# A gated linear-attention block: the second head's scores-times-values moved to the other two quarters of TensorE's array

## The chip, the cores and the metric

The kernel runs on one core of a Trainium2 chip. The metric is the device time of one execution in microseconds (us), as the median of several runs. The names of the engines in profiles are PE (TensorE's matmuls), PEld (TensorE's weight loads), DVE (VectorE), ACT (ScalarE), POOL (GpSimd) and SP (SyncE, which issues the DMAs).

## The reference, cut to what matters

One encoder block over 16 meta tokens and 1024 tokens with 1024 channels: a norm, a wide input projection, a pooling mixer, a gated linear attention, gates that merge the two, an output projection, and a squared-ReLU MLP. The change touches the attention. It has four heads with 64 key channels and 128 value channels, and goes in chunks of 64 tokens:

```python
def gla_chunk_step(S, inp):
    qc, kc, vc, ac = inp
    b = jnp.cumsum(ac, axis=2)
    decay = jnp.exp(-jnp.abs(b[:, :, :, None, :] - b[:, :, None, :, :]))
    scores = jnp.einsum('bhtk,bhsk,bhtsk->bhts', qc, kc, decay)
    o = jnp.einsum('bhts,bhsv->bhtv', scores, vc) + jnp.einsum('bhtk,bhkv->bhtv', qc * jnp.exp(b), S)
    b_end = b[:, :, -1:, :]
    S_new = jnp.exp(b_end[:, :, 0, :])[..., None] * S + jnp.einsum('bhsk,bhsv->bhkv', kc * jnp.exp(b_end - b), vc)
    return S_new, o
...
    o = rmsnorm(o, gla_norm.reshape(GLA_HEADS, GLA_DV)) * jax.nn.silu(r).reshape(B, L, GLA_HEADS, GLA_DV)
```

So the output o of a chunk is the masked and decayed scores times the values of the same chunk, plus the decayed queries times the state from the chunks before. It is normed over the 128 value channels of each head and multiplied by a gate made from r.

## The kernel before, in words

**Stages.** The program goes through the input projections for gates and queries (to about 208 us), the pooling mixer, then the attention (about 310 to 490 us), the merge with the output projection (to about 615 us) and the two MLP products (to the end). Most products of float32 operands are made as three matmuls of split operands (lines 255 to 257, the helper mm3); the attention's own are plain float32 matmuls, each of which the trace holds as two records of PE.

**The attention.** The heads go in pairs p (two heads e = 0, 1) and the tokens in halves of 512, so there are four units, in the order (0,0), (1,0), (0,1), (1,1) for (p, half). A unit has four token tiles j of 128, and each token tile has two chunks u of 64. A unit passes through `inside` (line 1210), which makes the masked scores `scc` level by level (score matmuls of line 1207 into the buffer b_sc, masked copies of line 1270), and then through `across` (line 1277). The `across` of one unit runs beside the `inside` of the next.

**The steps of `across`.** Line 1287 turns the decayed keys. Line 1296 multiplies keys by values into the two-bank buffer m2 (b_m in the trace), and line 1302 carries the states through the eight chunks on VectorE, reading that buffer. Line 1309 multiplies the scores by the values into the next b_m; since there is one such buffer, it waits for the last line 1302. Line 1314 (`seen`) reads one column of the result, so that the accumulation of line 1319 (queries times states, into the same places) comes after line 1309. Then come the squares (1328), their sums (1331), the norm's root (218 to 228), the multiply by it (1333), eight transposes to channels on partitions (1337), the multiply by the gate r in `sr` (1338, one instruction over 1024 columns), and the split of the product into two float32r parts for the merge (1340 on ScalarE, 1341 on VectorE).

**The quarters of the array.** All these matmuls have 64 rows of contraction and 64 columns of output. `tile_position=(row, column)` puts such a matmul on one 64 by 64 quarter of the array: the row says which partitions the operands come from, the column to which half of the partitions the result goes. In line 1309 the scores and values of chunk u lie on partition half u, and the result of token half u goes to partition half u, for both heads: positions (0, 0) and (64, 64). Lines 1207, 1296 and 1319 use all four positions in turn.

**The order of the work.** PE's order is written out in the program: `gla` (line 1344) steps through the generators, and each `yield us` pours as many microseconds of filler matmuls (key, value and gate projections, then the merge's products of `yb_block`, line 1088) before the next step. The other engines' orders are not written by hand at first, and are from `early_gates` (line 1073) on, which comes ahead of the last unit's `across`: from there ScalarE's and VectorE's instructions run in the order of the program. In that last stretch (the tail) the merge's products (lines 1115 and 1116, the rounding of line 1119, the remainder of lines 1121 and 1123 on VectorE or GpSimd) stand between the steps of the last unit, and the output weights (lines 1414, 1422, 1423) and the merge's weights (lines 83 and 87) are loaded and split.

Of the kernel before, what the change touches and what calls it, by code (L numbers as in the profile page):

```python
# [12 lines left out]
ALU = mybir.AluOpType  # L13
# [7 lines left out]
HALF = 512  # L21
CH = 64
# [92 lines left out]
def kernel(  # L115
# [10 lines left out]
    act, dve, pool, pe = nc.scalar, nc.vector, nc.gpsimd, nc.tensor  # L126
# [20 lines left out]
    def bank(tag):  # L147
        if tag in rota:
            turn_of[tag] = turn_of.get(tag, -1) + 1
            tag = rota[tag][turn_of[tag] % len(rota[tag])]  # L150
        return psp[tag].tile([P, 512], F32, name=f"b_{tag}", tag=tag)

    def two(tag):

        if tag == "sc":
            if "sc" not in wide:
                wide["sc"] = psp["sc"].tile([P, 2, 512], F32, name="b_sc", tag="sc")
            return wide["sc"]
        return psp[tag].tile([P, 2, 512], F32, name=f"b_{tag}", tag=tag)
# [40 lines left out]
    def f32(ap):  # L200
        return ap.bitcast(F32)
# [11 lines left out]
    def inv_sqrt(ss, n, inv, bias=None):  # L213

        rows, cols = ss.shape[0], n
        k = inv_sqrt.k = (inv_sqrt.k + 1) % 2
        v, y = stat[2 * k][:rows, 0:cols], stat[2 * k + 1][:rows, 0:cols]
        t = stat[2 * k][:rows, 8 : 8 + cols]
        act.activation(y, ss, ACT.Ln, scale=inv, bias=eps_t[:rows] if bias is None else bias)
        dve.tensor_scalar(v, ss, inv, EPS if bias is None else bias, ALU.mult, ALU.add)  # L220
        act.activation(y, y, ACT.Exp, scale=-0.5)
        if cols == 1:
            dve.scalar_tensor_tensor(t, v, y, y, ALU.mult, ALU.mult)
        else:
            dve.tensor_tensor(t, v, y, ALU.mult)
            dve.tensor_tensor(t, t, y, ALU.mult)
        dve.tensor_scalar(t, t, -0.5, 1.5, ALU.mult, ALU.add)
        dve.tensor_tensor(ss, y, t, ALU.mult)
        return ss
# [29 lines left out]
    def quad(a):  # L259
        return a.rearrange("p (k c) -> p k c", k=4)  # L260
# [934 lines left out]
    def part(i):  # L1195
        return slice(i * CH, (i + 1) * CH)
# [80 lines left out]
    def across(p, half):  # L1277


        v = S["v"][p][:, 4 * half : 4 * half + 4].rearrange("p j (e c) -> p j e c", e=2)  # L1280
        qe, kt, kl, W = (S[n] for n in ("qe", "kt", "kl", "W"))
        scc = S["scc"][:, p]
        dec = S["ends"][:, HALF - 2 * NC : HALF - NC]
        first = S["S"][:, half, p]
        yield 1.5
        b = quad(bank("ms"))
        for j in range(4):
            pe.transpose(b[:, j], kl[:, j * P : (j + 1) * P], ident)
        act.activation(kt, b, ACT.Copy)
        yield 1.6  # L1290
        while p and "v" not in done:
            yield 1.0
        kv = two("m2").rearrange("p u (j c) -> p u j c", j=4)
        for j in range(4):
            for u, e in ((0, 0), (1, 1), (1, 0), (0, 1)):
                pe.matmul(
                    kv[part(e), u, j], kt[part(u), j, part(e)], v[part(u), j, e], start=True, stop=True,
                    tile_position=(u * CH, e * CH),
                )
        states = [first] + [W[:, c] for c in range(NC - 1)] + ([S["S"][:, 1, p]] if half == 0 else [])  # L1300
        for c, dst in enumerate(states[1:]):
            dve.scalar_tensor_tensor(dst, states[c], dec[:, c : c + 1], kv[:, c % 2, c // 2], ALU.mult, ALU.add)
        yield 4.4

        o = two("m2").rearrange("p e (j c) -> p e j c", j=4)
        for j in range(4):
            for e in range(2):
                for u in range(2):
                    pe.matmul(  # L1309
                        o[part(u), e, j], scc[part(u), e, j], v[part(u), j, e], start=j == 0, stop=False,  # L1310
                        tile_position=(u * CH, u * CH), skip_group_check=True,
                    )

        dve.tensor_copy(seen, o[:, :, 3, P - 1])
        yield 0.8
        for j in (3, 0, 1, 2):
            for e, u in ((0, 0), (1, 1), (1, 0), (0, 1)):
                c = 2 * j + u
                pe.matmul(
                    o[part(u), e, j], qe[part(e), part(c)], states[c][part(e)], start=False, stop=True,  # L1320
                    tile_position=(e * CH, u * CH), skip_group_check=True,
                )
        while "v" not in done:
            yield 1.0
        sr = S["sr"].rearrange("p e t -> p (e t)")
        nc.sync.dma_start(sr.rearrange("p (e t) -> p e t", e=2), r_dram[2 * p : 2 * p + 2, half].rearrange("h p t -> p h t"))
        on, o = S["on"], o.rearrange("p e j c -> p (e j) c")
        act.activation(on, o, ACT.Square)
        ss = rms[rms_n[0] % 2]
        rms_n[0] += 1  # L1330
        dve.tensor_reduce(ss, on, AX.X, ALU.add)
        rs = inv_sqrt(ss, 8, 1.0 / P)
        dve.tensor_tensor(on, o, rs[:, :, None].broadcast_to([P, 8, P]), ALU.mult)
        yield 6.0
        b = two("m2").rearrange("p e (j c) -> p (e j) c", j=4)
        for j in range(8):
            pe.transpose(b[:, j], on[:, j], ident)
        dve.tensor_tensor(sr, b.rearrange("p a c -> p (a c)"), sr, ALU.mult)
        yh, yl = (S["yg"][half][:, n, 2 * p : 2 * p + 2].rearrange("p e t -> p (e t)") for n in range(2))
        act.activation(yh, sr, ACT.Copy)  # L1340
        dve.tensor_tensor(yl, sr, f32(yh), ALU.subtract)
        done.add((p, half))

    def gla():
# [16 lines left out]
        for n, u in enumerate(units + [None]):  # L1361
            if u is None:
                early_gates()
            live = side + old + ([inside(*u, units[n - 1] if n else None)] if u else [])
            while live:
                waits = [(g, next(g, None)) for g in live]
                live = [g for g, w in waits if w is not None]
                pour(max([w for _, w in waits if w is not None], default=0) * PACE)
                if not live:
                    break  # L1370
            if n == 2:
                done.add(("o", 0))
            if n == 0:
                while ("k", 1) not in done:
                    next(filler)
            old = [across(*u)] if u else []
            side = [meta_state(1)] if n == 0 else []
# [403 lines left out]
```

## Time and profile before

| | us |
|---|---|
| median of 3 runs | 1224.9 (1224.36 to 1225.51) |
| the profiled execution, its whole time | 1225.56 |
| its span | 1222.7 |
| PE busy | 1202.0 |
| VectorE busy | 853.9 |
| ScalarE busy | 618.9 |
| busy time of line 1309's matmuls, all four units | 7.86 |
| busy time of line 1319's matmuls, all four units | 4.42 |
| busy time of line 1338 on VectorE, all four units | 4.9 |

The profiled execution's time is its span and what lies around it. All times inside the program are counted from the span's start. Busy times of PE are modelled at their ends, since matmuls are pipelined. A row of the timeline reads: start, length, engine, line, operation, output <- inputs, shapes, count, and in brackets the idle time of the engine just before with what ended it. A row of a line's view reads: shortest, median and longest length in ns, then the first and last start.

### The profile page before, as it was taken

What the parts mean: (1) busy time and instruction counts of PE and PEld (TensorE: products, weight loads), DVE (VectorE), ACT (ScalarE), POOL (GpSimd) and SP (SyncE); (2) the same over time, 40 slices, a digit from 0 to 9 for tenths busy, and PEclk for the clock granted to TensorE, in tenths of its full rate; (3) what the DMA queues carried; (4) which work ended last, traced back from release to release, by engine and by line L of the source; (5) the groups of instructions that cost most, each with busy time, mean ns of one, the idle gap of its engine ahead of it and who ended that gap; (6) DMA issues with size and microseconds to landing.
All of it is one profiled execution on the core that took longest, in us unless ns stands there. A gap on an engine that the chain in (4) does not pass through costs nothing.

```text
span 1222.7 us, 18359 instructions
## 1 busy us (share of the span) xinstructions
PE 1202.0 (98%) x6818; PEld 1000.4 (82%) x6818; DVE 853.9 (70%) x1399; ACT 618.9 (51%) x1099; POOL 62.7 (5%) x100
## 2 busy tenths in 40 slices
PE   7999999999999999999999999999999999999997
PEld 7878888978888877788878888888888888888886
DVE  7986675754566677735887676676775887887686
ACT  7667567322546753323655455454554444444544
POOL 2000000001201225000000000000000000000000
PEclk9999999999999999999999999999999999999999
DMA  8043426156101246651244454444569973333532
GB/s 254 2 113 116 125 86 190 53 161 201 36 20 62 70 159 213 234 179 63 104 144 155 134 168 147 155 155 139 175 223 322 341 249 102 96 95 95 171 96 86
DMA packets 141672, 173.84 MB, mean 142 GB/s; under 512 B 9944, under 2 KB 81392, under 8 KB 141584
## 3 DMA queue, kind: packets, MB, share of 16 engines
q1 hardware_dynamic: 141552, 172.62, 43.6%
q8 instruction: 53, 0.87, 0.3%
q14 instruction: 35, 0.29, 0.1%
q0 software_dynamic: 32, 0.07, 0.0%
HBM read 119.17 MB, written 53.48 MB: 141 GB/s over the span
## 4 chain that ended last, share of the span: by engine, by line
PE 87%; DVE 7%; ACT 2%; issue 2%; DMA 1%; POOL 0%; SPq 0%; DVEq 0%; ACTq 0%; POOLq 0%
PE b_mm L255 10%; PE b_mm L256 10%; PE b_mm L257 10%; PE b_ms L256 9%; PE b_ms L255 9%; PE b_ms L257 9%; PE b_x L256 8%; PE b_x L255 8%; PE b_x L257 8%; PE b_sc L1207 1%; PE b_mx L255 1%; PE b_mx L256 1%; PE b_mx L257 1%; PE b_m L1309 1%; DVE ut L776 1%
## 5 line engine op out<-in xcount | busy, mean ns | idle before, releaser
L255 PE MATMUL b_mm<-th,w1h 128*128 128x512 f32 (+1 forms) x312 | 117.6, 377 | 1.6 <-DVE c L811 1.0
L256 PE MATMUL b_mm<-tl,w1h 128*128 128x512 f32 (+1 forms) x312 | 116.0, 372 | 0.6 <-DVE tl L1484 0.6
L257 PE MATMUL b_mm<-th,w1l 128*128 128x512 f32 (+1 forms) x312 | 115.9, 371 | 0.0
L255 PE MATMUL b_x<-th,w1h 128*128 128x512 f32 (+1 forms) x240 | 90.8, 378 | 0.0
L256 PE MATMUL b_x<-tl,w1h 128*128 128x512 f32 (+1 forms) x240 | 90.6, 378 | 0.0
L257 PE MATMUL b_x<-th,w1l 128*128 128x512 f32 (+1 forms) x240 | 90.3, 376 | 0.0
L273 ACT ACTIVATE w1h<-raw 128x512 fp32r<-128x512 f32 x96 | 59.5, 621 | 32.6 <-PE b_x L256 14.2
L274 DVE TENSOR_TENSOR w1l<-raw,w1h 128x512 fp32r<-128x512 f32 x96 | 65.6, 684 | 9.9 <-ACT w1h L273 9.9
L255 PEld LDWEIGHTS b_mm<-th,w1h 128*128 128x128 f32 x312 | 58.6, 188 | 13.2 <-issue 1.4
L273 ACT ACTIVATE w1h<-fs 128x512 fp32r<-128x512 f32 x72 | 45.4, 630 | 46.3 <-PE b_ms L256 31.8
L256 PEld LDWEIGHTS b_mm<-tl,w1h 128*128 128x128 f32 x312 | 58.6, 188 | 10.7 <-DVE tl L1484 0.9
L257 PEld LDWEIGHTS b_mm<-th,w1l 128*128 128x128 f32 x312 | 58.6, 188 | 10.3
L273 ACT ACTIVATE w1h<-bt 128x512 fp32r<-128x512 f32 x44 | 27.8, 632 | 67.1 <-issue 62.7
L274 DVE TENSOR_TENSOR w1l<-fs,w1h 128x512 fp32r<-128x512 f32 x72 | 49.3, 686 | 14.7 <-ACT w1h L273 14.6
L1638 DVE TENSOR_TENSOR bt<-w,w 128x512 f32<-128x512 f32 x80 | 54.6, 683 | 1.6 <-DMA w<-in_w_ff_dram 1.6
L257 PEld LDWEIGHTS b_x<-th,w1l 128*128 128x128 f32 x240 | 45.1, 188 | 8.5
L255 PEld LDWEIGHTS b_x<-th,w1h 128*128 128x128 f32 x240 | 45.1, 188 | 8.4
L256 PEld LDWEIGHTS b_x<-tl,w1h 128*128 128x128 f32 x240 | 45.1, 188 | 8.3
L273 ACT ACTIVATE fxh<-bt 128x512 fp32r<-128x512 f32 x36 | 22.8, 632 | 55.7 <-issue 50.1
L255 PE MATMUL b_ms<-wo,w1h 128*128 128x512 f32 x128 | 49.8, 389 | 0.0
L256 PE MATMUL b_ms<-wo,w1h 128*128 128x512 f32 x128 | 49.8, 389 | 0.0
L257 PE MATMUL b_ms<-wo,w1l 128*128 128x512 f32 x128 | 49.8, 389 | 0.0
(451 smaller groups left out, 3349.2 us busy)
## 6 DMA issues: line engine op xcount, KB each, us to landing
hf_dram<-h SPq DMA_DIRECT2D x112, 256.0 KB, 2.1
raw<-hf_dram SPq DMA_DIRECT2D x112, 256.0 KB, 2.6
w<-in_w_ff_dram SPq DMA_DIRECT2D x64, 256.0 KB, 4.7
raw<-in_w_in_dram SPq DMA_DIRECT2D x24, 512.0 KB, 4.8
raw<-in_w_ff_dram SPq DMA_DIRECT2D x16, 512.0 KB, 4.1
rawx<-in_w_ff_dram SPq DMA_DIRECT2D x16, 512.0 KB, 4.0
xs<-in_x_dram SPq DMA_DIRECT2D x8, 512.0 KB, 5.6
rawx<-in_w_in_dram SPq DMA_DIRECT2D x8, 512.0 KB, 4.4
```

The costliest lines, as they stand in the source:

```text
L255: pe.matmul(ps, ah, bh, start=first and i == 0, stop=False, skip_group_check=more)
L256: pe.matmul(ps, ah, bl, start=False, stop=False, skip_group_check=more)
L257: pe.matmul(ps, al, bh, start=False, stop=last and i == n - 1, skip_group_check=more)
L273: act.activation(hi, a, ACT.Copy)
L274: dve.tensor_tensor(lo, a, f32(hi), ALU.subtract)
L776: dve.tensor_tensor(to_, a_, b_, ALU.subtract)
L1207: pe.matmul(b[to, e, j], kk[r, s], qq[r, s], start=True, stop=True, tile_position=(e * CH, u * CH))
L1309: pe.matmul(o[part(u), e, j], scc[part(u), e, j], v[part(u), j, e], start=j == 0, stop=False, tile_position=(u * CH, u * CH), skip_group_c ...
L1638: dve.tensor_tensor(bt, w, S["w2"][q[3:]][:, i], ALU.add if q[2] == "+" else ALU.subtract)
```

## The change

In line 1309 head e = 1 takes the other two quarters: the operands stay where they are, and the result of token half u goes to partition half 1 - u (`u ^ e`). The accumulation of line 1319 follows the result to its new place, and goes through (e, u) in another order. The square, the sums, the root and the norm's multiply work on each partition by itself and are as before. After the transposes the second head's token halves stand swapped along the columns, and the gate multiply reads them swapped: one multiply over the first head's 512 columns, and two over the second head's, each over 256 columns in four runs of 64.

```diff
             for e in range(2):
                 for u in range(2):
                     pe.matmul(
-                        o[part(u), e, j], scc[part(u), e, j], v[part(u), j, e], start=j == 0, stop=False,
-                        tile_position=(u * CH, u * CH), skip_group_check=True,
+                        o[part(u ^ e), e, j], scc[part(u), e, j], v[part(u), j, e], start=j == 0, stop=False,
+                        tile_position=(u * CH, (u ^ e) * CH), skip_group_check=True,
                     )
...
         for j in (3, 0, 1, 2):
-            for e, u in ((0, 0), (1, 1), (1, 0), (0, 1)):
+            for e, u in ((0, 0), (1, 0), (1, 1), (0, 1)):
                 c = 2 * j + u
                 pe.matmul(
-                    o[part(u), e, j], qe[part(e), part(c)], states[c][part(e)], start=False, stop=True,
-                    tile_position=(e * CH, u * CH), skip_group_check=True,
+                    o[part(u ^ e), e, j], qe[part(e), part(c)], states[c][part(e)], start=False, stop=True,
+                    tile_position=(e * CH, (u ^ e) * CH), skip_group_check=True,
                 )
...
-        dve.tensor_tensor(sr, b.rearrange("p a c -> p (a c)"), sr, ALU.mult)
+        in_tiles = lambda a: a.rearrange("p (j u c) -> p j u c", j=4, u=2)
+        dve.tensor_tensor(sr[:, :HALF], b[:, :4].rearrange("p a c -> p (a c)"), sr[:, :HALF], ALU.mult)
+        for u in range(2):
+            to = in_tiles(sr[:, HALF:])[:, :, u]
+            dve.tensor_tensor(to, b[:, 4:8, part(1 - u)], to, ALU.mult)
```

## The prediction

> **What bounds the kernel now.** I read the page first: busy shares, then the chain that ended last.
>
> ```profile
> span 1222.7 us, 18359 instructions
> PE 1202.0 (98%) x6818; PEld 1000.4 (82%) x6818; DVE 853.9 (70%) x1399; ACT 618.9 (51%) x1099; POOL 62.7 (5%) x100
> PE 87%; DVE 7%; ACT 2%; issue 2%; DMA 1%; POOL 0%; SPq 0%; DVEq 0%; ACTq 0%; POOLq 0%
> ```
>
> TensorE is busy for 98% of the span and carries 87% of the chain; VectorE has 7%. But busy time is a mean over stages, so I asked next for the stretch that holds the edit (the recurrence, 300 to 490 us) and for what comes after it. The columns are length, then busy time with count for PE, PEld, DVE, ACT, POOL, then granted clock and DMA.
>
> ```profile
> 300.00:490.00 190.00, 188.90 (x2111) 157.44 (x2111) 122.08 (x238) 102.77 (x180) 45.20 (x56) 1.00 0.28 92
> 512.00:630.00 118.00, 115.61 (x538) 95.36 (x539) 76.33 (x135) 50.46 (x97) 0.00 (x0) 1.00 0.38 131
> 630.00:920.00 290.00, 290.00 (x1281) 240.18 (x1280) 207.03 (x326) 150.39 (x251) 0.00 (x0) 1.00 0.50 164
> ```
>
> In the recurrence PE lacks only 1.1 us of 190, in the feed-forward nothing, and the clock is full throughout. PE's order is written out and filler projections are poured between the steps, so a microsecond taken from PE here is a microsecond off the end unless something outside PE holds the next step. What PE waits for after 300 us is the third view (total, times, longest).
>
> ```profile
> PE b_mm L256 <- DVE wo L1423: 0.8, 1, 0.8
> PE b_sc L1207 <- DVE scc L1270: 0.6, 1, 0.6
> PE b_mm L256 <- DVE yg L1341: 0.3, 1, 0.3
> PE b_m L1309 <- DVE W L1302: 0.2, 1, 0.2
> ```
>
> The waits are short and end on VectorE or ScalarE; none ends on a DMA. So the gain can only be lost where a VectorE chain, not PE, sets the pace. Three such places are weighed below.
>
> **The change on PE.** Line 1309 is issued four times, once for each unit (p, half), as 16 matmuls that the trace holds as 32 records. Before, they use the two diagonal quarters of the array: e=0 and e=1 both go (0,0), (64,64). After, e=1 goes to (0,64), (64,0), so four quarters are in use. Line 1319 already issues 16 matmuls of the same size over all four. Windows limited to one line give each block's busy time, which is its length from first start to last end: first L1309 (one unit, then the sum over four), then L1319 (one unit and sum).
>
> ```profile
> 355.00:358.00 3.00, 1.96 (x32) 1.72 (x32) 1.00 0.00 0
> sum 36.00, PE 7.86 PEld 6.93; mean PE 0.65 PEld 0.58
> 360.00:362.00 2.00, 1.10 (x32) 0.86 (x32) 1.00 0.00 0
> sum 36.00, PE 4.42 PEld 3.45; mean PE 0.37 PEld 0.29
> ```
>
> Two quarters take 1.96 us for 32 records, four take 1.10. So L1309 should fall to 1.10: 0.86 us a unit, 7.86 - 4.42 = **3.44 us in all**. The second hunk only follows the new places: in the loop over L1319 its reordering of (e, u) gives the same sequence of quarters as before, (0,0), (64,64), (64,0), (0,64); cost nothing, and the block's other operands are ready long before. What L1309's own length used to cover is the copy L1314 behind it and the next L1207; both lie after L1309 in PE's order and wait on work done earlier, so they move with it.
>
> One thing differs from the four-quarter blocks. In L1319 each row group writes a bank of its own (both follow e). In the changed L1309 each row group writes both banks. The narrow windows of the timeline show what starts together, 20 ns of L1309 and 40 ns of L1319:
>
> ```profile
> 355.67 0.33 PE L1309 MATMUL b_m<-v,scc 64*64 64x128 f32 x2
> 360.19 0.34 PE L1319 MATMUL b_m<-W,mix 64*64 64x128 f32 x4
> ```
>
> The two of L1309 are e=0, u=0 and u=1: two row groups writing bank 0 at once, in different partition halves, and they run together. The four of L1319 put two banks under each column group at once. The changed block combines just these two, so I take 1.10 us. Bounds: 1.10 below, 1.96 above (pairs at a time). The Trainium skill, "TensorEngine Tiling (Array Packing)", Gotcha 1: PSUM Pressure, says that different row tiles cannot access the same PSUM bank simultaneously. By that rule the block would stay at 1.96 us; the first row above speaks against it in this form, since two row tiles start within 20 ns on one bank.
>
> **The change on VectorE.** The 1024-column gate multiply L1338 becomes one of 512 and two of 256 columns, the latter in runs of 64: 8 instructions more in all, in place in the same tile, no DMA and no new queue.
>
> ```profile
> L1338 DVE TENSOR_TENSOR mix<-b_m,mix x4: 1214/1220/1225, 373.8 to 481.1; 128x1024 f32<-128x1024 f32 x4
> L1115 DVE TENSOR_TENSOR t<-b_mm,t x9: 676/683/692, 457.9 to 515.2; 128x512 f32<-128x512 f32 x9
> L1252 DVE TENSOR_TENSOR mix<-n,ends x8: 406/416/424, 332.2 to 453.7; 128x256 f32<-128x256 f32 x8
> 414.84 0.75 DVE L1252 TENSOR_TENSOR mix<-n,ends 128x256 f32<-128x256 f32 x2
> 408.61 0.89 PE b_m L1337 x8
> ```
>
> Two strided 256-column pieces back to back take 0.75, not 0.83: consecutive ones overlap by 0.08. So 0.68 + 0.75 - 0.08 = 1.35 to 1.36 us against 1.22: **+0.14 us** a unit. Upper bound without overlap: 0.683 + 2 x 0.416 - 1.220 = +0.29. Lower bound: where VectorE idles for the transposes, the first piece needs only four of the eight and could start up to some 0.4 us earlier (half of the eight's 0.89), so about -0.25. I take +0.14, which the row of two such pieces shows. What it does in each unit:
>
> Unit (0,0): behind L1338 stands ScalarE's L1340, then L1341.
>
> ```profile
> 374.45 0.88 ACT L1231 ACTIVATE n<-kq 128x512 f32<-128x512 f32 x1 [0.23 <-PE b_sc L1207]
> 375.24 1.04 ACT L1340 ACTIVATE yg<-mix 128x1024 fp32r<-128x1024 f32 x1
> 376.31 1.23 DVE L1341 TENSOR_TENSOR yg<-mix,yg 128x1024 fp32r<-128x1024 f32 x1 [0.36 <-ACT yg L1340]
> ```
>
> L1338 ends at 373.8 + 1.22 = 375.0, ScalarE is at L1231 until 375.24: a cover of 0.2 us, and VectorE waits 0.36 afterwards. Nothing is paid; without that cover it would be 0.14.
>
> Unit (1,0): L1338 starts a chain that is VectorE's or ScalarE's almost without a gap until the states are done, and the next L1309 needs the buffer that they read.
>
> ```profile
> 394.79 0.35 DVE L1302 SCALAR_TENSOR_TENSOR S<-W,ends,b_m 128x128 f32<-128x128 f32 x1
> 395.28 0.33 PE L1309 MATMUL b_m<-v,scc 64*64 64x128 f32 x2
> 409.52 1.23 DVE L1338 TENSOR_TENSOR mix<-b_m,mix 128x1024 f32<-128x1024 f32 x1 [1.68 <-PE b_m L1337]
> 433.14 0.73 DVE L1302 SCALAR_TENSOR_TENSOR W<-W,ends,b_m 128x128 f32<-128x128 f32 x2
> 434.01 0.33 PE L1309 MATMUL b_m<-v,scc 64*64 64x128 f32 x2 [0.15 <-DVE W L1302]
> ```
>
> At 434.01 PE waits 0.15 us for L1302, and at 395.28 it starts 0.14 us after L1302's end, just as at 434.01: VectorE is level with PE there. Both chains begin at PE's transposes L1337 and so move forward with PE, but each delay inside them is paid: +0.14 at 434. Unit (0,1) has no L1309 wait behind it: nothing.
>
> Unit (1,1), the tail, with the step that starts it:
>
> ```profile
> 469.96 0.69 DVE L1115 TENSOR_TENSOR t<-b_mm,t 128x512 f32<-128x512 f32 x1 [0.79 <-PE b_mm L257]
> 470.26 1.06 ACT L83 ACTIVATE w1h<-raw 128x1024 fp32r<-128x1024 f32 x1 [0.19 <-DMA raw<-in_w_gla_out_dram]
> 472.96 0.63 ACT L1119 ACTIVATE th<-t 128x512 fp32r<-128x512 f32 x1 [1.64 <-DVE t L1116]
> 480.51 0.69 DVE L1116 TENSOR_TENSOR t<-t,o 128x512 f32<-128x512 f32 x1
> 481.12 1.22 DVE L1338 TENSOR_TENSOR mix<-b_m,mix 128x1024 f32<-128x1024 f32 x1
> 482.37 1.06 ACT L1340 ACTIVATE yg<-mix 128x1024 fp32r<-128x1024 f32 x1 [0.50 <-DVE mix L1338]
> 483.46 1.52 DVE L1341 TENSOR_TENSOR yg<-mix,yg 128x1024 fp32r<-128x1024 f32 x1 [1.13 <-ACT yg L1340]
> 487.05 3.73 POOL L1123 TENSOR_TENSOR tl<-t,th 128x256 fp32r<-128x256 f32 x4 [3.15 <-ACT th L1119]
> 512.64 0.50 PE L256 MATMUL b_mm<-wo,th 128*128 128x512 f32 x1 [0.76 <-DVE wo L1423]
> ```
>
> Here L1338 is behind a busy VectorE, L1340 and L1341 follow it at once, then the merge's products, POOL's L1123, SP's fetch of the output weights, and at last PE at 512.64: +0.14, paid in full. What starts this chain, L1115 at 469.96, is released by PE's fillers just after L1309 of this unit, so it comes 3.44 us earlier as well.
>
> Sum: -3.44 + 0 + 0.14 + 0 + 0.14 = **-3.16 us**, which from 512.64 on goes straight to the end, as PE has no wait on a transfer there. The profiled execution took 1225.56 us (its span of 1222.7 and 2.86 around it), 0.66 above the median of 1224.9. 1225.56 - 3.16 = 1222.4; beside the median, **1221.7 us**. About 0.2%, 2.45 us, is what a measurement can tell from no change, so the forecast stands only a little beyond that.
>
> **The rivals.**
>
> *A held tail.* The chain from 470 us could keep an anchor that does not move by the whole 3.44. ScalarE's L83 at 470.26 waits for a weight transfer, issued when earlier W1 work freed its buffer, before the last L1309; it gains from three units only, 2.58. If ScalarE then set the pace: -2.58 + 0.28 = -2.3, or 1222.6; with stretched VectorE work beside POOL (the 1.52 of L1341 is 0.3 above L1341's 1.23 in the first unit) up to some 1224.6. For it: the 0.19 wait. Against: ScalarE then idles 1.64 us before L1119, more than the 0.86 at stake.
>
> *The banks serialize.* Row groups that share a bank take turns, the four quarters again go two at a time, L1309 keeps 1.96, and the change does not do what it says: only +0.28 is left, 1225.2. This is the time that the rule from the Trainium skill named above would give. For it: no four-quarter block here writes this way. Against: the pair at 355.67.
>
> *VectorE's order, the slower side.* VectorE's order before the tail is not written by hand: L1341 follows L1252 in unit (0,0) but L1239 in (1,0). If the split multiply's last piece is put behind a copy L1270 that waits for the next scores, L1340 and all behind it slip by one level of filler. How long that is shows in the chain of waits, between two blocks of scores with fillers between them:
>
> ```profile
> 451.30 0.64 PE b_sc L1207 x32
> 454.22 0.64 PE b_sc L1207 x32
> ```
>
> Place: the chains to L1309 at 395 and 434, where VectorE is level with PE. Price: 2.9 us each, 5.8 + 0.28 - 3.44 = +2.6, 1227.5. It decides the sign once the two slips sum to more than 3.2. Against: the pieces have no input that the whole did not have.
>
> *More than forecast.* The early start pays at 434 (0.15 is all PE can collect there) or less VectorE time is stretched by POOL: 1219.5 to 1220.9.
>
> **How the numbers follow.** Forecast (1220.9 to 1222.4) 0.60; more 0.07; held tail 0.18, of which 0.02 still beyond 0.2%; banks 0.05; order 0.10. Faster by over 0.2%: 0.60 + 0.07 + 0.02 = 0.69. Within: 0.16 + 0.05 = 0.21. Slower: 0.10. Range: the forecast, the held tail to its end and part of "more": 1220.2 to 1224.6, leaving out the banks, the order and a few hundredths. VectorE's bounds (at most 0.15 a unit more, or 0.15 less at 434) lie inside the forecast's own range.
>
> **What would show it.** L1309: 1.10 us busy in each unit, four records starting within some 30 ns; if 1.96, the banks. L1338: one row near 683 ns and two near 416, with L1340 some 0.14 later behind its start. PE's wait at the second and third L1309 at most 0.3; above 1 us, the order. PE's start behind L1423 (now 512.64) near 509.5 in the span; if it is near 510.4 or later while the fourth L1309 is 2.4 to 2.6 earlier, the tail. A wait of PE on a transfer anywhere after 300 us would make the sum wrong.

## The result, and the profile after

The changed kernel takes 1222.43 us (median of 14 runs, 1222.15 to 1223.36) against 1225.12 us before in the same set: 2.69 us less, a ratio of 0.9978 with a 95% interval of 0.9971 to 0.9986. By its median that is just beyond the 0.2% that the forecast takes for the least that can be told from no change; the interval reaches to both sides of it. The profiled execution took 1222.45 us with a span of 1220.3.

First the shares of the engines. TensorE has lost 2.8 us of busy time, and it still carries the chain.

```profile
span 1220.3 us, 18368 instructions
PE 1199.2 (98%) x6818; PEld 997.7 (82%) x6818; DVE 854.7 (70%) x1407; ACT 619.0 (51%) x1099; POOL 62.2 (5%) x100
PE 87%; DVE 7%; ACT 2%; issue 2%; DMA 1%; POOL 0%; SPq 0%; DVEq 0%; ACTq 0%; POOLq 0%
```

Then line 1309 alone, in windows around its four places (length, PE busy, PEld busy, clock, DMA), and a window of 50 ns at its first start:

```profile
355.00:358.00 3.00, 1.10 (x32) 0.86 (x32) 1.00 0.00 0
394.00:398.00 4.00, 1.10 (x32) 0.89 (x32) 1.00 0.16 19
432.00:435.00 3.00, 1.10 (x32) 0.89 (x32) 1.00 0.18 68
464.00:467.00 3.00, 1.10 (x32) 0.86 (x32) 1.00 0.66 208
sum 13.00, PE 4.42 PEld 3.51; mean PE 1.10 PEld 0.88
```

```profile
356.18 0.34 PE L1309 MATMUL b_m<-v,scc 64*64 64x128 f32 x4
```

Four records start at once where two did, and each block takes 1.10 us where it took 1.96. The starts also show how: within a block a new set follows every 0.11 us in both kernels, sixteen sets of two before, eight sets of four now. The gate multiply, by shape (count, then busy time and mean ns), is two new groups; the ScalarE step behind it is now line 1344, the VectorE step after that line 1345.

```profile
L1342 DVE TENSOR_TENSOR mix<-b_m,mix 128x256 f32<-128x256 f32 x8 | 3.0, 415 | 0.0
L1339 DVE TENSOR_TENSOR mix<-b_m,mix 128x512 f32<-128x512 f32 x4 | 2.7, 687 | 3.3 <-PE b_m L1337 3.3
```

Where the time went is best seen by following PE itself: its 6818 records are in the same order in all kernels here (but for the inner order of lines 1309 and 1319), so the start of the same record can be compared between two traces. The table gives PE's start minus that in the kernel before, in us (negative is earlier), at five places of the kernel before's time: ahead of the first L1309 (355.0), behind the fourth (469.0), at the last unit's transposes (479.0), behind the output weights that end the tail (513.0), and at PE's last record. The last two columns are differences of the first ones: what the four L1309 brought, and what the tail took back.

| kernel | 355 | 469 | 479 | 513 | end | four L1309 | tail to 513 |
|---|---|---|---|---|---|---|---|
| changed | +0.51 | -2.80 | -2.65 | -2.24 | -2.35 | -3.31 | +0.57 |
| changed, second profile | +0.41 | -2.95 | -1.83 | -1.75 | -1.17 | -3.36 | +1.20 |
| changed, third profile | +0.48 | -2.86 | -2.52 | -2.44 | -2.59 | -3.34 | +0.41 |

So the PE part comes out to a few hundredths each time. Two things eat at it: half a microsecond that is lost within the first 10 us of the span, where the change has no part, and the tail, where the loss is another in each execution. A third place, behind 513, moves PE either way (the second profile loses another 0.58 there); it is looked at in the section on the prediction.

What the tail does in the first of these profiles, by rows of VectorE, ScalarE, SP and PE:

```profile
467.76 1.49 DVE L1427 TENSOR_TENSOR wo<-raw,wo 128x1024 fp32r<-128x1024 f32 x1
468.45 1.06 ACT L83 ACTIVATE w1h<-raw 128x1024 fp32r<-128x1024 f32 x1 [1.17 <-DMA raw<-in_w_gla_out_dram]
469.88 0.63 ACT L1119 ACTIVATE th<-t 128x512 fp32r<-128x512 f32 x1 [0.37 <-DVE t L1116]
472.72 0.55 DVE L220 TENSOR_SCALAR small<-small 128x8 f32<-128x8 f32 x1
473.37 0.59 DVE L225 TENSOR_TENSOR small<-small 128x8 f32<-128x8 f32 x1
478.47 0.68 DVE L1339 TENSOR_TENSOR mix<-b_m,mix 128x512 f32<-128x512 f32 x1
479.07 0.75 DVE L1342 TENSOR_TENSOR mix<-b_m,mix 128x256 f32<-128x256 f32 x2
479.85 1.06 ACT L1344 ACTIVATE yg<-mix 128x1024 fp32r<-128x1024 f32 x1 [0.63 <-DVE mix L1342]
488.17 0.38 SPq L1418 DMA_DIRECT2D acc<-in_w_out_dram  x1
492.73 1.06 ACT L1426 ACTIVATE wo<-acc 128x1024 fp32r<-128x1024 f32 x1 [0.91 <-DMA o<-ma_dram]
510.41 0.50 PE L256 MATMUL b_mm<-wo,th 128*128 128x512 f32 x1 [0.77 <-DVE wo L1427]
```

L83 came only 1.81 us earlier than before (470.26), since it starts when its weights land and they landed only that much earlier; ScalarE's spare time ahead of L1119 shrank from 1.64 to 0.37 us, but L1119 itself is 3.08 us earlier, so nothing was lost there. L225, a multiply of eight columns, took 0.59 us here, beside GpSimd, which worked from 472.49 to 473.93. In the kernel before GpSimd was done at 476.31, and the same instruction was through in 0.17. The rows of the kernel before for this step and for the output weights:

```profile
476.44 0.17 DVE L225 TENSOR_TENSOR small<-small 128x8 f32<-128x8 f32 x1
490.81 0.38 SPq L1414 DMA_DIRECT2D acc<-in_w_out_dram  x1
494.96 1.06 ACT L1422 ACTIVATE wo<-acc 128x1024 fp32r<-128x1024 f32 x1 [0.50 <-DMA t<-gb_dram]
```

That is 0.42. Behind it the multiply costs its split: L1344 starts 1.38 us after L1339's start where L1340 started 1.25 after L1338's, +0.13. And the output weights' fetch was issued 2.64 us earlier than before (490.81, the kernel before's L1414) while ScalarE could start on them only 2.23 earlier (494.96 before): +0.4 in the transfer. (The brackets of these two rows name other transfers, but in both traces ScalarE starts 0.2 us after the last part of this fetch has landed.) These three make 0.96; the table has 0.57, because two things went better than in the kernel before: L1116, which GpSimd had stretched to 1.23 us there, took 0.68, against L1427 with 1.49 instead of 1.21, and L1345 took 1.39 instead of 1.52.

### The profile page after: what moved, and what is told of

The parts are those of the page before. It is cut to its first block, busy times and chain, and to the rows that moved or that the text cites. A ratio compares the mean times of both kernels' runs of the same rounds, so it can differ in the third digit from the quotient of the medians.

```text
span 1220.3 us, 18368 instructions
## 1 busy us (share of the span) xinstructions
PE 1199.2 (98%) x6818; PEld 997.7 (82%) x6818; DVE 854.7 (70%) x1407; ACT 619.0 (51%) x1099; POOL 62.2 (5%) x100
## 4 chain that ended last, share of the span: by engine, by line
PE 87%; DVE 7%; ACT 2%; issue 2%; DMA 1%; POOL 0%; SPq 0%; DVEq 0%; ACTq 0%; POOLq 0%
PE b_mm L255 10%; PE b_mm L256 10%; PE b_mm L257 10%; PE b_ms L255 9%; PE b_ms L257 9%; PE b_ms L256 9%; PE b_x L256 8%; PE b_x L255 8%; PE b_x L257 8%; PE b_sc L1207 1%; PE b_mx L255 1%; PE b_mx L256 1%; PE b_mx L257 1%; DVE ut L776 1%; DVE t L1115 1%
## 5 line engine op out<-in xcount | busy, mean ns | idle before, releaser
L273 ACT ACTIVATE w1h<-raw 128x512 fp32r<-128x512 f32 x96 | 59.5, 620 | 32.9 <-PE b_x L256 14.2
L273 ACT ACTIVATE w1h<-fs 128x512 fp32r<-128x512 f32 x72 | 45.4, 630 | 45.7 <-PE b_ms L256 31.2
L273 ACT ACTIVATE w1h<-bt 128x512 fp32r<-128x512 f32 x44 | 27.8, 632 | 66.6 <-issue 62.2
L273 ACT ACTIVATE fxh<-bt 128x512 fp32r<-128x512 f32 x36 | 22.8, 632 | 56.3 <-issue 50.7
```

Source lines behind the costliest of these rows:

```text
L273: act.activation(hi, a, ACT.Copy)
```

## The experiments

The theory: each L1309 gives PE about 0.84 us because four quarters work instead of two, and all of it is kept up to the tail; the tail gives back 0.13 us for the split and a varying amount because VectorE, GpSimd and transfers meet at other moments. The rivals: banks have a part in the 1.96 or the 1.10; the split costs more than its length; the tail holds whatever comes early.

All medians are against the kernel before in the same set.

**The changed kernel again.** No edit.

> The changed kernel once more, for the scatter. Two readings of the 0.6 us that the profile of the changed kernel is short of the 3.35 us that L1309 gave on PE. Arrival: the tail (470 to 500 us) meets GpSimd and the weight transfer at other moments when PE comes 3.3 us earlier; PE's start behind L1337 and behind the second merge weights falls back by 0.1 to 0.6 us again, and the whole is 2.6 to 2.9 us faster than before. Split: the three-piece multiply costs it, the same numbers here, told apart by the next two kernels. The extra 0.5 us at 8 to 10 us of the span (the first transposes at half pace) should be gone or different if it is scatter of one execution, and the same if it comes with the program.

Measured: 1222.66 against 1224.87, -2.21 us, ratio 0.9982 (0.9973 to 0.9991): less of a gain than the 2.6 to 2.9 expected. The half microsecond at the start was there again (+0.41 by 355). The tail took 1.20, most of it ahead of the split multiply:

```profile
465.46 1.26 DVE L1116 TENSOR_TENSOR t<-t,o 128x512 f32<-128x512 f32 x1 [0.84 <-DMA o<-ma_dram]
468.36 1.60 DVE L1427 TENSOR_TENSOR wo<-raw,wo 128x1024 fp32r<-128x1024 f32 x1 [0.66 <-ACT wo L1426]
469.88 1.22 DVE L1116 TENSOR_TENSOR t<-t,o 128x512 f32<-128x512 f32 x1
```

```profile
PE b_m L1337 <- DVE mix L1333: 1.1, 1, 1.1
```

VectorE waits 0.84 us for a transfer that the first profile did not wait for, then ScalarE's L1426 is late, and L1116 takes 1.22 us beside GpSimd (0.68 in the first profile, but 1.23 in the kernel before); PE ends up waiting 1.1 us at its transposes. The same program, another 0.6 us in the tail: it is scatter.

**The PE part alone.** The result's second head keeps its halves exchanged.

```diff
-        in_tiles = lambda a: a.rearrange("p (j u c) -> p j u c", j=4, u=2)
-        dve.tensor_tensor(sr[:, :HALF], b[:, :4].rearrange("p a c -> p (a c)"), sr[:, :HALF], ALU.mult)
-        for u in range(2):
-            to = in_tiles(sr[:, HALF:])[:, :, u]
-            dve.tensor_tensor(to, b[:, 4:8, part(1 - u)], to, ALU.mult)
+        dve.tensor_tensor(sr, b.rearrange("p a c -> p (a c)"), sr, ALU.mult)
```

> The changed kernel with the old gate multiply in one piece (this leaves out the swap back, so the second head's token halves stay exchanged in the result). It is the PE part of the change alone. Split theory: all of the shortfall goes, 3.2 to 3.4 us faster than before. Arrival theory: only the 0.13 us of the split in the tail comes back, 2.7 to 3.0 us faster than before, and L225 or L1116 is still stretched beside GpSimd and PE still falls back at the second merge weights.

Measured: 1221.92, -2.95 us, 0.9974 (0.9964 to 0.9983). On PE: +0.29 at the start, -3.38 by the four L1309, +0.21 in the tail. The 2.95 lies in the arrival theory's range and short of the split theory's. L225 was stretched (0.58 us) as in the changed kernel's first profile, so that is not the split's doing. But the changed kernel in the same set is 0.74 behind, where the arrival theory allows 0.13.

**The split alone**, in the kernel before.

```diff
-        dve.tensor_tensor(sr, b.rearrange("p a c -> p (a c)"), sr, ALU.mult)
+        in_tiles = lambda a: a.rearrange("p (j u c) -> p j u c", j=4, u=2)
+        dve.tensor_tensor(sr[:, :HALF], b[:, :4].rearrange("p a c -> p (a c)"), sr[:, :HALF], ALU.mult)
+        for u in range(2):
+            to = in_tiles(sr[:, HALF:])[:, :, u]
+            dve.tensor_tensor(to, b[:, 4:8, part(u)], to, ALU.mult)
```

> The kernel before with the gate multiply in three pieces (256-column pieces in runs of 64, no swap). Arrival theory: 0.1 to 0.3 us slower than before (0.13 in the tail, at most as much again at the third L1309). Split theory: 0.5 to 0.7 us slower than before.

Measured: 1225.59, +0.72 us, 1.0005 (0.9995 to 1.0014). By the medians this is the split theory's number and not the arrival theory's; the interval is too wide to choose. The trace says more: PE is within 0.07 us of the kernel before through all four units and gets 0.18 late in the tail; another 0.18 comes after 513, at the start of the MLP, where the kernel is the same.

**The exchange in the transposes.** The four transposes of the second head read the identity with its column halves exchanged, so the gate multiply is one instruction again and the result is whole.

```diff
+        swapped = bass.AP(ident.tensor, ident.offset + CH, (ident.ap[0], (-CH, 2), (1, CH)))
         for j in range(8):
-            pe.transpose(b[:, j], on[:, j], ident)
+            pe.transpose(b[:, j], on[:, j], swapped if j > 3 else ident)
...
+        dve.tensor_tensor(sr, b.rearrange("p a c -> p (a c)"), sr, ALU.mult)
```

> The changed kernel, but the second head's token halves are exchanged in the transposes (the moving operand is the identity read with its column halves exchanged), so the gate multiply stays in one piece and the result is the reference's. If a moving operand in two runs costs PE nothing, it is like the PE part alone: 2.7 to 3.0 us faster than before by arrival, 3.2 to 3.4 by split. If the four transposes read slower, some 0.1 us each time, 0.2 to 0.4 us less of a gain.

Measured: 1221.88, -2.99 us, 0.9976 (0.9966 to 0.9985), as the PE part alone. The transposes cost what they did; this is their group here (line 1338), and the changed kernel's line 1337 has the same 4.2 us and 275 ns:

```profile
L1338 PE MATMUL b_m<-ident,mix 128*128 128x128 f32 x32 | 4.2, 275 | 0.3 <-DVE mix L1333 0.3
```

**Three units, and the last unit alone.** The change is switched by a number x that is 1 in the chosen units.

```diff
+        x = int((p, half) != (1, 1))
...
-                        o[part(u ^ e), e, j], scc[part(u), e, j], v[part(u), j, e], start=j == 0, stop=False,
-                        tile_position=(u * CH, (u ^ e) * CH), skip_group_check=True,
+                        o[part(u ^ (e & x)), e, j], scc[part(u), e, j], v[part(u), j, e], start=j == 0, stop=False,
+                        tile_position=(u * CH, (u ^ (e & x)) * CH), skip_group_check=True,
```

> The change in the units (0,0), (1,0) and (0,1) alone; the last unit is as before, gate multiply included. Additive theory: PE is 3 x 0.84 = 2.5 us early when it comes to the tail and keeps it within the scatter of the tail (0.1 to 1.2 us lost in the runs so far): 1.6 to 2.5 us faster than before. Held tail: what the last unit adds was lost anyway, so the whole is no less fast than the changed kernel.

> The change in the last unit alone. Additive theory: its L1309 takes 1.10 instead of 1.96 us, PE is 0.84 to 0.86 early behind it, and the split gate multiply in the tail gives 0.13 back: 0.4 to 0.8 us faster than before. Held tail: nothing is kept beyond L1423, within 0.2 us of before.

Measured: three units 1222.41, -2.91 us, 0.9977 (0.9967 to 0.9986); the last alone 1224.5, -0.82 us, 0.9995 (0.9986 to 1.0005). On PE the three units bring -2.53, the last -0.84, which add up to the -3.3 to -3.4 of the whole. At PE's last record the three units are -2.54; the last unit alone, -0.46 behind its L1309, is +0.22 at the end, after 0.25 in the tail and 0.43 later. The three units' 2.91 is more than the 1.6 to 2.5 that was expected. By the medians three units are worth as much as four, by PE's steps at L1309 0.8 less: the intervals allow both. What the last unit's share is worth at the end is therefore not shown; that it arrives at the tail is.

**The order of the quarters.** The changed kernel with the loops over u and e exchanged, so that neighbours share a row group and not a bank.

```diff
-            for e in range(2):
-                for u in range(2):
+            for u in range(2):
+                for e in range(2):
```

> The changed kernel with L1309's loops exchanged: the quarters come in the order (0,0), (0,64), (64,64), (64,0), so the two that share a row group, not the two that share a bank, start next to each other. If each quarter has a queue of its own and banks cost nothing, L1309 is 1.10 us busy per unit as before the exchange. If two matmuls that read the same rows cannot go side by side and the order hid that, it rises towards 1.96.

Measured: L1309 is 4.42 us busy, 1.10 a unit, as in the changed kernel; 1222.34 us in its single run, on PE -3.39 over the four.

```profile
300.00:490.00 190.00, 4.42 (x128) 3.51 (x128) 1.00 0.29 93
```

**The banks of the two quarters.** The kernel before with this edit alone: the two matmuls that run side by side, which write one bank there, now write different ones.

```diff
-            for e in range(2):
-                for u in range(2):
+            for e, u in ((0, 0), (1, 1), (1, 0), (0, 1)):
```

> The kernel before (two diagonal quarters) with the matmuls of L1309 reordered so that neighbours in time write different banks: (e,u) = (0,0), (1,1), (1,0), (0,1). Quarters theory: two quarters set the pace, L1309 stays at 1.96 us per unit. Bank theory (row groups on one bank take turns, part of the 1.96 is that): it falls below 1.96.

Measured: 7.86 us busy, 1.96 a unit, unchanged, and PE within 0.05 us of the kernel before from the first L1309 to 513; 1225.37 us in its single run. (After 513 PE loses 0.51 all the same.)

```profile
300.00:490.00 190.00, 7.86 (x128) 6.95 (x128) 1.00 0.29 92
```

The bank theory falls on both sides: neither does sharing a bank cost the pair anything, nor does sharing a row group cost the four. What counts in these blocks is how many quarters are in use.

**A second set: the changed kernel, the exchange in the transposes, and a gate multiply in two pieces.** The last reads the halves of each token tile in reverse in one instruction:

```diff
-        for u in range(2):
-            to = in_tiles(sr[:, HALF:])[:, :, u]
-            dve.tensor_tensor(to, b[:, 4:8, part(1 - u)], to, ALU.mult)
+        to, e1 = in_tiles(sr[:, HALF:]), b[:, 4:8]
+        e1 = bass.AP(e1.tensor, e1.offset + CH, (e1.ap[0], (P, 4), (-CH, 2), (1, CH)))
+        dve.tensor_tensor(to, e1, to, ALU.mult)
```

> The changed kernel once more, beside the two kernels below on one chip. By the PE steps seen so far (0.82, 0.83, 0.84, 0.86 at the four L1309) less 0.13 for the split in the tail, 3.2 us less whatever the tail and the start of this execution scatter: median 2.2 to 3.2 us below before.

> The exchange in the transposes once more. If the split's only cost is its 0.13 us in the tail, it is 0.1 to 0.2 us faster than the changed kernel; if the 0.8 us between their medians in the first set was more than scatter, it is that again.

> The changed kernel with the gate multiply in two pieces of 512 columns: the second head's piece reads each token tile's halves in reverse order in one instruction. 0.61 + 0.68 us against 1.22 in one and 1.36 in three pieces: +0.07 instead of +0.14 us in the tail. Two rows of VectorE near 0.68 us at that line; the median between the other two, not to be told apart from them.

Measured: the changed kernel 1222.88, -2.26 us, 0.9981 (0.9972 to 0.9990); the exchange in the transposes 1222.17, -2.97 us, 0.9975 (0.9965 to 0.9984); two pieces 1221.94, -3.2 us, 0.9977 (0.9967 to 0.9986). The piece that reads in reverse is as quick as a plain one:

```profile
L1341 DVE TENSOR_TENSOR mix<-b_m,mix 128x512 f32<-128x512 f32 x4 | 2.7, 681 | 0.0
```

The exchange in the transposes is 0.7 to 0.8 us below the changed kernel in both sets, more than the split's 0.13 explains; the intervals overlap. The recorded runs show where a part of it lies. Each has its whole time and the span of its instructions; what is left around the span has a median of 2.12 to 2.18 us in the kernels with three pieces in all units (the changed kernel in its three sets, the split alone), of 1.81 to 1.87 in those with one multiply (the PE part, the exchange twice), and of 1.78 and 1.90 in the kernel before in two of these sets. So some 0.3 us lies outside the first to last instruction, where no step of the tail can be its cause; why, the runs do not show. By the medians of the spans alone the exchange is 0.15 and 0.3 us ahead of the changed kernel.

**Where the rest of that sits.** The split in three units, the exchange in the transposes in the last.

```diff
+            pe.transpose(b[:, j], on[:, j], swapped if j > 3 and (p, half) == (1, 1) else ident)
...
+        if (p, half) != (1, 1):
...
+        else:
+            dve.tensor_tensor(sr, b.rearrange("p a c -> p (a c)"), sr, ALU.mult)
```

> The changed kernel with the split gate multiply in the first three units and the exchange in the transposes (one multiply) in the last. The changed kernel's medians were 2.2 to 2.7 us below before, those with one multiply everywhere 2.9 to 3.0; 0.13 of that is the split in the tail. If the rest sits in the tail as well (the split moves what follows against GpSimd and the transfers), this kernel is 2.9 to 3.0 below before. If it sits in the first three units, 2.3 to 2.7, though there the traces showed no loss. If it was scatter between jobs, anything from 2.3 to 3.0, and it stays open.

Measured: 1222.62 against 1225.41, -2.79 us, 0.9976 (0.9966 to 0.9986): between the two answers. The traces say a little more. From 469 to 513 the five profiles with PE over 2 us early and a multiply in pieces in the last unit lost 0.41 to 1.20 us (the changed kernel 0.57, 1.20, 0.41, the row order 0.47, two pieces 0.83), the five with one multiply there 0.09 to 0.35 (the PE part 0.21, the exchange 0.22 and 0.09, three units 0.35, this one 0.32). So a multiply in pieces goes with a tail some 0.4 us longer, of which 0.13 is its own length. But a good part of the 1.20 was lost ahead of that multiply, the two pieces with their 0.83 have the best median of all (-3.2), where PE is hardly early a tail with pieces takes only 0.18 and 0.25 (the split alone, the last unit alone), and five profiles of each kind are few: by what means the rest would come is open.

## Why the prediction was right, and where it was off

The forecast was 1221.7 us, 3.16 us less, with a range from 1220.2 to 1224.6; measured were 1222.43 and -2.69, at the upper edge of the forecast's own 1220.9 to 1222.4. The mechanism on PE was right; the way from there to the end was taken too simply. That the two profiled executions differ by 3.11 us, almost the forecast's 3.16, is luck: the span shrank by 2.4, and the time around it happened to fall from 2.86 to 2.15. By its steps:

- **L1309 falls to 1.10 us, 3.44 us in all.** Busy time went from 7.86 to 4.42, exactly as the rows of L1319 had it. PE's later records moved 3.31 to 3.41 us, a little less: behind the last block 0.86, behind the first three 0.79 to 0.82, where the kernel before had the first scores (396.87) start ahead of the block's last two matmuls (396.94).
- **The second hunk costs nothing.** The rows of L1319 are unchanged (1.10 us a unit).
- **The split costs +0.14.** The pieces took 0.687 and 0.415 us and overlapped as forecast; the step behind them came 0.13 later. The early start that the lower bound allowed did not happen: L1339 still waited for all eight transposes.
- **+0.14 at the third L1309.** This was not paid. The order of two of ScalarE's instructions changed there; before, then after:

```profile
415.82 0.85 ACT L1231 ACTIVATE f<-kq 128x512 f32<-128x512 f32 x1
416.58 0.58 ACT L920 ACTIVATE t<-b_mm 128x512 f32<-128x512 f32 x1
417.19 0.63 ACT L921 ACTIVATE t<-t 128x512 f32<-128x512 f32 x1
```

```profile
414.85 0.57 ACT L920 ACTIVATE t<-b_mm 128x512 f32<-128x512 f32 x1
415.33 0.85 ACT L1231 ACTIVATE f<-kq 128x512 f32<-128x512 f32 x1
416.09 0.61 ACT L921 ACTIVATE t<-t 128x512 f32<-128x512 f32 x1
```

  L920 goes ahead of the second L1231: L921 starts 1.10 us earlier than before although the chain reached this place (L1253) only 0.98 us earlier. PE's wait at L1309 stayed at 0.2 us. This comes with the split: L920 is ahead in all seven profiles that have three pieces in that unit and in none of the other seven. The rival of VectorE's order had seen that an order not written by hand may change with the edit; it was ScalarE's that did, and it paid 0.12 instead of costing.
- **+0.14 in the tail.** This term was too small. The tail gave back 0.41 to 1.20 us instead. The held-tail rival was partly right in its size (it allowed up to 1224.6) and wrong in its place: L83 did come late, 1.81 instead of 3.44 us earlier, but did not set the pace. What did were single instructions stretched beside GpSimd (L225, L1427), a transfer that VectorE had to wait for (L1116's operand from ma_dram) and one that took 0.4 us longer (the output weights), different ones in each execution. None of these can be read from one profile of the kernel before, which has its own draw of them (its L1116 at 471.7 took 1.23 us). PE's start behind the output weights, forecast near 509.5, came at 510.41: 0.43 of this is the tail, 0.51 the start of the program.
- **From 512.64 on straight to the end, as PE has no wait on a transfer there.** This step failed. PE itself has no such wait after 300 us in any of the profiles, but it has one by way of two other engines. At the start of the MLP PE waits for ScalarE's L1483, which waits for VectorE, which works without a gap from L324 on, and L324 waits for feed-forward weights. First the kernel before, then the kernel of the two quarters' banks, which was level with it up to here:

```profile
606.61 0.69 DVE L324 TENSOR_TENSOR fs<-rawx 128x512 f32<-128x512 f32 x1 [0.54 <-DMA rawx<-in_w_ff_dram]
615.28 0.49 PE L255 MATMUL b_mm<-th,w1h 128*128 128x512 f32 x1 [0.61 <-ACT th L1483]
```

```profile
607.02 0.69 DVE L324 TENSOR_TENSOR fs<-rawx 128x512 f32<-128x512 f32 x1 [0.87 <-DMA rawx<-in_w_ff_dram]
615.69 0.50 PE L255 MATMUL b_mm<-th,w1h 128*128 128x512 f32 x1 [0.98 <-ACT th L1482]
```

  In all fourteen profiles PE starts there 8.67 or 8.68 us after L324, whose wait for the transfer is anything from 0.30 to 0.88 us. So PE's time from here on is that of a landing, and what the tail kept is changed once more: between 513 and the end PE moved by -0.28 to +0.59 us over the thirteen profiles taken after the prediction. Most of that is in this one step; four of them lose 0.14 to 0.35 more at 630, behind a second wait of this kind (ScalarE's L273). The 0.54 us of waiting stood in the profile before.
- **Banks.** The fear that row groups sharing a bank take turns was unfounded here, from both sides (the two orders above).

The start of the program, +0.3 to +0.5 us in six of these thirteen profiles, belongs to no step. It lies ahead of all that the change touches, one of the six has the change in the last unit alone, and the changed kernel in the row order does not have it (+0.04). All three profiles of the changed kernel do, though, and that this is chance is not shown.

## What to carry to other kernels

Count the quarters, not the matmuls: a block of sixteen 64 by 64 matmuls on two quarters of the array took 1.96 us here and on four 1.10, and a neighbour of the same size in the same trace gave the price of the other layout to the hundredth. When the layout of a result changes for that, look for an instruction that already moves data through an address pattern (here a transpose's identity, or one reversed read) to undo it, before adding instructions on another engine. And when a gain arrives at a stretch that is bound by short steps of several engines and transfers, expect a few tenths of it to be lost there, other ones in each run. A view that shows no wait of PE on a transfer does not say that none sets its pace: follow each wait back through the engines in between.

## What the runs showed of the hardware that was not expected

The half microsecond at the start is TensorE at half pace. Windows from 7.9 to 9.9 us, first the kernel before, then the changed kernel's third profile (busy time and count for PE, PEld, DVE, ACT, POOL, then granted clock):

```profile
7.90:9.90 2.00, 2.00 (x20) 2.00 (x19) 1.24 (x3) 1.88 (x5) 0.00 (x0) 1.00 1.21 311
```

```profile
7.90:9.90 2.00, 2.00 (x11) 2.00 (x10) 0.79 (x2) 1.48 (x4) 0.00 (x0) 1.00 1.18 302
```

In the same 2 us the one execution gets 20 transposes through and the other 11. In each the transposes start 0.21 us apart at first and 0.11 apart later; the pace changes at 8.1 us in the kernel before and at 11.2 in the other. The clock column reads 1.00 in both windows, but it counts a stretch without an entry as full. In the trace's own record of the granted clock the first entry, full clock, stands at 8.12 and at 11.23 us, just where the pace changes. In the six profiles with the late start it stands at 9.3 to 11.2, in the other eight at 8.1 to 9.2. The Trainium skill, "TensorE: Matmul & The Clock Gate", Part 1: The HAM clock gate, says that the array starts at half rate until a window of activity has passed, and that the window runs freely, so that the number of slow matmuls differs from run to run. The traces agree: the same first records, at half pace for another length of time.

A moving operand read with its halves in reverse order costs a transpose nothing (275 ns a record either way), and a VectorE operand read so costs a multiply nothing (681 ns against 687 for the plain piece beside it). The eight-column multiply L225 took 0.59 us with GpSimd at work and 0.17 without.
